# The recurrent branch's output product as seven products of halves, with its tokens kept in quads and its weight sums formed in DRAM

## The chip, the cores and the metric

The kernel runs on one core of a Trainium2 chip. It computes one decoder block for 512 tokens, and its time is the device time of one execution in microseconds. Before the change the median of three runs is 703.79 us (703.75 to 704.28).

Five engines work side by side, each on its own list of instructions in a fixed order: PE (TensorE, matrix products), DVE (VectorE), ACT (ScalarE), POOL (GpSimd) and SP (SyncE, which here only issues transfers). An instruction waits at the head of its engine's list until what it needs is there, and all behind it wait too. Transfers (DMAs) are issued by an engine and then run on their own. Matrix products read their operands from SBUF and write to PSUM, which has eight banks of 128 x 512 numbers.

## The reference

Only the part of the block up to the first residual sum is touched:

```python
h = rms_norm(x, g_mix_pre)
z = h @ w_in                       # (512, 1024) @ (1024, 4608): pool, rnn x, rnn gate, two gates
y_pool = pool_mixer(u_pool, pool_w, pool_scale) @ w_pool_out         # 512 -> 1024
y_rnn = rg_lru_branch(u_rx, u_rg, ...) @ w_rg_out                    # 1024 -> 1024
merged = gate_pool * y_pool + gate_rnn * y_rnn
x = x + rms_norm(merged @ w_o, g_mix_post)
```

`rg_lru_branch` ends with `h * gelu(gb)`, a scan's output times a gate. After this part come the feed-forward network (`w_up`, a short convolution, `w_down`) and a per-layer embedding. All is in float32.

## The kernel before, in words

**Precision.** PE multiplies in a shorter format (fp32r) than float32, so each operand is split into two: `hi`, a copy of it that ACT casts, and `lo`, the remainder that DVE subtracts (`split`, L190 and L194; L435 for weights that stream in). A product is three products, hi x hi, hi x lo and lo x hi, into one bank (`mm3`, L220 to L222).

**Layout.** A tile is 128 x 512 numbers: 128 channels by all 512 tokens. A weight tile of 512 KB (128 x 1024) serves one product of 128 output channels over 1024 inputs: eight blocks by three matmuls of 512 columns, 24 in all.

**Seven products of halves.** The products with `w_o`, `w_up` and `w_down` are already done so that a product of 2 x 2 blocks takes seven block products in place of eight. The sums of weight blocks that this needs (forms 5, 6, 7 and 4; forms 1, 2 and 3 are plain blocks) are made in DRAM: POOL issues a copy of a block to a sum tensor and then a transfer that adds another block to it (`sums_of`, `sum_in_dram`, L295). The sums of activations are DVE subtractions.

**Stages around the change.** The in-projection's last 24 steps (`IN_ORDER`) are 16 gate tiles, four pool tiles and four small maps. Then a loop over m = 0 to 7 makes, for 128 output channels each, `y_pool @ w_pool_out` (12 matmuls, key `wpo`) and `y_rnn @ w_rg_out` (24 matmuls, key `wrg`), and three DVE instructions (L879 to L881) multiply both by their gates and add them. Then the products with `w_o` follow, in the order of `SERIAL`.

**What sets the order.** PE's order is that of the program. The other engines' lists are laid by a scheduler from the program and from priorities (`urgent` puts an instruction ahead of others). Weights stream through six buffers each for `raw`, `hi` and `lo`; `weight` starts a tile's load, cast and subtraction four tiles ahead of its use. All loads are issued by SP, in one list.

**Early splits.** Ten weight tiles that are used later (six of `w_o`, four of `w_up`) are loaded, split and written back to DRAM as `parts` ahead of time (`split_early`), and read back when needed: one at each of the in-projection's last four steps (`EARLY_AT` = 20), and one in each of the loop's first six passes. Each takes a 512 KB load and two 512 KB writes on SP's list, a cast on ACT, a subtraction on DVE, and a `hi` and a `lo` buffer that come free when the writes have landed.

## Time and profile before

| | |
|---|---|
| median of the runs | 703.79 us |
| profiled execution: span / its own time | 702.1 us / 703.83 us |
| PE busy | 696.5 us (99%) |
| DVE busy / ACT busy / POOL busy | 574.1 / 440.9 / 82.9 us |
| moved by DMA | 172.54 MB |

The span runs from the first to the last instruction in the profile; 1.73 us lie around it. Times of day in what follows are microseconds from the span's start. The last gate tile ends and the loop over m begins at 203 us; the products with `w_o` begin at 265 us. A busy time is the time in which an engine has an instruction under way; matmuls overlap, so the distance between two starts, not the length of one, is the price of a matmul in a row of them.

### The profile page before, as it was taken

The numbers are of one execution on the slowest core, as the hardware profiler recorded it, in microseconds if no ns is written. First come the engines' busy times: TensorE is split into PE (matmuls) and PEld (weight loads), VectorE is DVE, ScalarE is ACT, GpSimd is POOL, SyncE is SP. The second block draws the span as 40 slices with busy tenths as digits, with TensorE's granted clock in tenths as the row PEclk, the third lists the DMA queues.
The fourth block names the chain that finished last, engine by engine and source line by source line (L and its number), as shares of the span: only waits on it lengthen the run. The fifth ranks groups of instructions, "written<-read, shape, count | busy, mean of one in ns | idle before, by whom it ended". The sixth has DMA issues, their size and how long they took to land.

```text
span 702.1 us, 11239 instructions
## 1 busy us (share of the span) xinstructions
PE 696.5 (99%) x4279; PEld 637.0 (91%) x4279; DVE 574.1 (82%) x749; ACT 440.9 (63%) x670; POOL 82.9 (12%) x107
## 2 busy tenths in 40 slices
PE   9999999999999999999999999999999999999997
PEld 8888888888888888899999999999999888888886
DVE  5698645999656568777989999997999999788972
ACT  6857789953543245468866667765767766665631
POOL 0221111110000000121013232121300000001100
PEclk9999999999999999999999999999999999999999
DMA  8999986656698999996479999998976577868111
GB/s 320 406 314 244 227 229 153 157 165 219 237 327 285 323 334 374 332 317 218 152 286 240 278 297 266 304 239 299 241 200 233 203 250 235 283 206 273 47 61 60
DMA packets 65077, 172.54 MB, mean 246 GB/s; under 512 B 5952, under 2 KB 6592, under 8 KB 64704
## 3 DMA queue, kind: packets, MB, share of 16 engines
q1 hardware_dynamic: 50480, 129.88, 53.2%
q0 software_dynamic: 14400, 41.95, 25.5%
q8 instruction: 33, 0.54, 0.3%
q14 instruction: 20, 0.16, 0.1%
q10 hardware_dynamic: 144, 0.00, 0.0%
HBM read 155.03 MB, written 58.72 MB: 304 GB/s over the span
## 4 chain that ended last, share of the span: by engine, by line
PE 99%; DVE 0%; ACT 0%; issue 0%
PE ps L220 31%; PE ps L222 31%; PE ps L221 31%; PE ps L541 3%; PE ps L913 1%; PE ps L650 1%; PE ps L239 1%; PE ps L592 0%; ACT t L165 0%; DVE t L1323 0%; DVE t L1324 0%; PE ps L1034 0%; DVE m L231 0%; DVE mhalf L233 0%
## 5 line engine op out<-in xcount | busy, mean ns | idle before, releaser
L190 DVE TENSOR_TENSOR lo<-raw,hi 128x1024 fp32r<-128x1024 f32 (+2 forms) x193 | 224.0, 1184 | 60.2 <-ACT hi L435 42.3
L220 PE MATMUL ps<-A,hi 128*128 128x256 f32 (+1 forms) x608 | 194.4, 320 | 0.0
L221 PE MATMUL ps<-A,hi 128*128 128x256 f32 (+1 forms) x608 | 193.8, 319 | 0.0
L222 PE MATMUL ps<-A,lo 128*128 128x256 f32 (+1 forms) x608 | 193.8, 319 | 0.0
L435 ACT CAST hi<-raw 128x1024 fp32r<-128x1024 f32 (+1 forms) x112 | 112.0, 1011 | 80.6 <-PE ps L222 27.6
L220 PEld LDWEIGHTS ps<-A,hi 128*128 128x128 f32 x608 | 115.9, 191 | 8.2 <-issue 1.0
L222 PEld LDWEIGHTS ps<-A,lo 128*128 128x128 f32 x608 | 116.0, 191 | 6.8
L221 PEld LDWEIGHTS ps<-A,hi 128*128 128x128 f32 x608 | 116.0, 191 | 6.8
L220 PE MATMUL ps<-C,hi 128*128 128x256 f32 (+1 forms) x392 | 114.5, 292 | 0.0
L222 PE MATMUL ps<-C,lo 128*128 128x256 f32 (+1 forms) x392 | 114.3, 292 | 0.0
L221 PE MATMUL ps<-C,hi 128*128 128x256 f32 (+1 forms) x392 | 114.3, 292 | 0.0
L194 ACT CAST hi<-raw 128x1024 fp32r<-128x1024 f32 x78 | 80.3, 1050 | 24.5 <-PE ps L221 14.5
L220 PE MATMUL ps<-hi,A 128*128 128x512 f32 x224 | 85.2, 380 | 0.0
L221 PE MATMUL ps<-lo,A 128*128 128x512 f32 x224 | 84.9, 379 | 0.0
L222 PE MATMUL ps<-hi,A 128*128 128x512 f32 x224 | 84.9, 379 | 0.0
L220 PEld LDWEIGHTS ps<-C,hi 128*128 128x128 f32 x392 | 74.7, 191 | 1.9
L221 PEld LDWEIGHTS ps<-C,hi 128*128 128x128 f32 x392 | 74.7, 191 | 1.8
L222 PEld LDWEIGHTS ps<-C,lo 128*128 128x128 f32 x392 | 74.7, 191 | 1.7
L462 POOL TENSOR_TENSOR s<-s,mhalf 128x1 f32<-128x1 f32 (+1 forms) x21 | 16.2, 773 | 336.9 <-DVE s L478 315.1
L220 PEld LDWEIGHTS ps<-hi,A 128*128 128x128 f32 x224 | 42.3, 189 | 6.3 <-ACT hi L435 0.3
L222 PEld LDWEIGHTS ps<-hi,A 128*128 128x128 f32 x224 | 42.3, 189 | 6.0
L221 PEld LDWEIGHTS ps<-lo,A 128*128 128x128 f32 x224 | 42.3, 189 | 5.8
(191 smaller groups left out, 1024.0 us busy)
## 6 DMA issues: line engine op xcount, KB each, us to landing
raw<-in_w_up_dram SPq DMA_DIRECT2D x46, 512.0 KB, 7.7
wdsum<-in_w_down_dram POOLq DMA_DIRECT2D x36, 512.0 KB, 9.2
raw<-in_w_in_dram SPq DMA_DIRECT2D x32, 512.0 KB, 6.9
raw<-wdsum SPq DMA_DIRECT2D x24, 512.0 KB, 4.5
raw<-in_w_down_dram SPq DMA_DIRECT2D x18, 512.0 KB, 4.0
wosum<-in_w_o_dram POOLq DMA_DIRECT2D x12, 512.0 KB, 9.0
wdsum<-wdsum POOLq DMA_DIRECT2D x12, 512.0 KB, 6.9
parts<-hi SPq DMA_DIRECT2D x10, 512.0 KB, 5.0
```

Of the source, the lines that this page charges most:

```text
L190: return V.tensor_tensor(o, a, b, ALU.subtract)
L194: last_copy[0] = ACT.copy(hi, src)
L220: PE.matmul(o, ah, bh, start=start, stop=False, **kw)
L221: PE.matmul(o, ah, bl, start=False, stop=False, **kw)
L222: PE.matmul(o, al, bh, start=False, stop=stop, **kw)
L239: PE.matmul(wps[:, :P], ones, ones, start=True, stop=True)
L435: ins = ACT.copy(hi, raw)
L462: last_pow[0] = nc.gpsimd.tensor_tensor(y, v, mhalf[:, :n], ALU.pow).ins.name
L541: PE.matmul(rx[m], a[:, o : o + P], turns(b), start=k == 0 and i == 0, stop=k == KD - 1 and i == 2)
L650: PE.matmul(ps, bd[pr, a, o], turns(b[pr]), start=i == 0, stop=i == 2)
L913: PE.transpose(ps[:, q * P : (q + 1) * P], a[:, q * P : (q + 1) * P], ident)
```

## The change

The product `y_rnn @ w_rg_out` becomes seven products of halves. Tokens are halved (256 each), and the output's 1024 channels are handled in two passes p = 0, 1 of 512. In each pass seven forms are multiplied, in the order `RSEVEN`; a form is two products (i = 0, 1) of four blocks by three matmuls of 256 columns, so that a pass has 168 matmuls. The weight tiles of forms 5, 6, 7 and 4 come from 16 more transfers on POOL's list, put ahead of those for `w_o`; the sums of p = 1, 2 of `w_up` are now issued side by side, as those of `w_rg_out` are.

The eight products with `w_pool_out` now stand in a row ahead of the fourteen forms. The output of the scan times its gate is written into two quads (`rgq`, four tiles each), and three DVE subtractions in them (`rg_sums`, at gate tiles 9 to 11) and one addition make the activation forms; forms 1 and 4 are split at gate tiles 5 and 8, the others in the `wpo` loop (`LATE_FORMS`). In PSUM the products collect in `rz`, `rd`, `ra` and `rb2`: ACT copies `rz` into `ra` and, negated, into `rb2` after forms 1, 6 and 7 (L938, L943, L945, L946), and `merge` does on DVE what L879 to L881 did, for halves.

Early splits start at step 15 in place of 20: nine lie in the in-projection's last nine steps, one in the `wpo` loop. The quarters of `w_o` take their input channels in another order, and the merged tokens lie in two quads `mq` to match. The two loads of `p_t` move from the loop's fourth pass to behind p = 0.

```diff
-EARLY_AT = 20
-SPLIT_AT = 5, 8
+EARLY_AT = 15
+FORMS_AT, RSUMS_AT = {5: 1, 8: 4}, (9, 10, 11)
...
+RSEVEN = (1, 5, 6, 2, 3, 7, 4)
...
+LATE_FORMS = {0: 5, 1: 6, 2: 3, 3: 7, 4: 2}
...
+    rsum = {(p, f): dram.tile([P, 2, S], F32, name=f"rg{p}sum{f}") for p in range(2) for f in (5, 6, 7, 4)}
...
+        if name in ("up", "rg"):
+            sums, of, ps = (usum, up_block, UP_SUMS) if name == "up" else (rsum, rg_block, range(2))
+            for fs in (((5, 11, 12), (7, 12, 22)), ((6, 5, 22),), ((4, 6, 21),)):
+                todo = [(p, *f) for f in fs for p in ps]
+                for p, f, start, _ in todo:
+                    yield sums[p, f], sums[p, start] if start < 10 else of(p, start), {}
+                for p, f, _, more in todo:
+                    yield sums[p, f], of(p, more), {"accum_op": ALU.add}
...
-    early = [("wo", f, q) for f in SERIAL[4:] for q in range(pieces["wo"])] + [("up", 0, f) for f in PLAIN]
+    early = [("wo", f, q) for f in SERIAL[4:] for q in range(pieces["wo"])]
+    early[2:2] = [("up", 0, f) for f in PLAIN]
...
-    sum_in_dram(chain_of(sums_of("wo"), sums_of("up")), None)
+    sum_in_dram(chain_of(sums_of("rg"), sums_of("wo"), sums_of("up")), None)
...
-            V.tensor_tensor(r_t[c], r_t[c], rg_t[c], ALU.mult)
+            V.tensor_tensor(rg_t[c], r_t[c], rg_t[c], ALU.mult)
...
+        w = quad("C" if f in (1, 2, 4) else "A").rearrange("p (s a) (b c) -> p s (a b) c", s=2, b=2)
+        split(w[:, 0], w[:, 1], v)
...
-    mq = [quad("A", F32), quad("A", F32)]
+    mq, pas = [], []
     for m in range(KD):
         w = weight(("wpo", m))
-        pa = bank()
+        if m in LATE_FORMS:
+            rg_form(LATE_FORMS[m])
+        if m == 6:
+            split_early(1)
+        pas.append(bank())
         for k in range(4):
-            mm3(pa, pick(w, k * P, (k + 1) * P), yp[k], k == 0, k == 3)
-        w = weight(("wrg", m))
...
-        for k in range(KD):
-            y = yh[k // 4][:, k % 4, :], yl[k // 4][:, k % 4, :]
-            mm3(pb, pick(w, k * P, (k + 1) * P), y, k == 0, k == KD - 1)
+            mm3(pas[m], pick(w, k * P, (k + 1) * P), yp[k], k == 0, k == 3)
...
+    def rg_product(p, f):
+        for i in range(2):
+            w = weight(("rg", p, f))
+            o = {1: rz, 6: rz, 7: rz, 2: ra, 4: ra, 3: rb2, 5: (rd, rd)}[f][i]
+            a = HALF if f == 4 or (f, i) == (5, 1) else 0
+            products(o[:, a : a + HALF], w, i, rform[f], f in (1, 5), turns)
+            z = rz[i][:, :HALF]
...
+                if f == 1:
+                    ACT.copy(ra[i][:, :HALF], z)
...
+                elif f == 7:
+                    ACT.copy(ra[i][:, HALF:], z)
+                    ACT.activation(rb2[i][:, HALF:], z, AF.Identity, scale=-1.0)
...
+    for p in range(2):
+        for f in RSEVEN:
+            if f == 2:
+                mq.append(quad("C", F32))
+            rg_product(p, f)
+            if (p, f) == (1, 6):
+                o_form(1)
+            if (p, f) == (1, 3):
+                o_form(2)
```

The change moves rows on SP, ACT and DVE. SP's list at the end of the in-projection and the start of the loop, first before: `parts` are the early tiles' writes, `raw` are loads.

```order
L428 DMA raw_1896<-in_w_rg_out_dram 128x1024
L428 DMA raw_1932<-in_w_pool_out_dram 128x512
L359 DMA parts_122<-hi_1848 128x1024
L359 DMA parts_122<-lo_1849 128x1024
L428 DMA raw_1951<-in_w_rg_out_dram 128x1024
L355 DMA raw_1957<-wosum_107 128x1024
L359 DMA parts_123<-hi_1890 128x1024
L359 DMA parts_123<-lo_1891 128x1024
L428 DMA raw_1993<-in_w_pool_out_dram 128x512
```

And the same place after, where raw_1823, raw_1865, raw_1907 and raw_1949 are the tiles of the `wpo` products m = 0 to 3:

```order
L373 DMA parts_133<-lo_1818 128x1024
L442 DMA raw_1823<-in_w_pool_out_dram 128x512
L369 DMA raw_1857<-wosum_106 128x1024
L442 DMA raw_1865<-in_w_pool_out_dram 128x512
L369 DMA raw_1899<-wosum_106 128x1024
L442 DMA raw_1907<-in_w_pool_out_dram 128x512
L373 DMA parts_134<-hi_1859 128x1024
L373 DMA parts_134<-lo_1860 128x1024
L373 DMA parts_135<-hi_1901 128x1024
L373 DMA parts_135<-lo_1902 128x1024
L369 DMA raw_1941<-wosum_107 128x1024
L442 DMA raw_1949<-in_w_pool_out_dram 128x512
```

The four writes of two early tiles and the load of a third now stand ahead of the load for m = 3, where before one tile's two writes stood between loads.

ACT's list at the end of the last gate tile, after: m_1938 and m_1980 are the last two gates' sigmoids, A_1989 and A_2012 forms 5 and 6, hi_1943 an early tile's cast, and hi_1951 the cast for m = 3.

```order
L166 ACTIVATE m_1938<-m_1938 128x512
L195 CAST A_1989<-C_406 128x1024
L195 CAST A_2012<-C_405 128x1024
L166 ACTIVATE m_1980<-m_1980 128x512
L195 CAST hi_1943<-raw_1941 128x1024
L449 CAST hi_1951<-raw_1949 128x512
L449 CAST hi_1985<-raw_1983 128x512
```

Two casts of forms, a sigmoid and an early cast now stand ahead of the cast for m = 3. The last place is ACT's list where the `w_o` products begin, first before: L994 copies `oz` of form 1 into `o11`, and A_2515 is the cast of form 5.

```order
L194 CAST A_2420<-A_1931 128x1024
L994 COPY ps_2450<-ps_2448 128x512
L435 CAST hi_2497<-raw_2495 128x1024
L994 COPY ps_2451<-ps_2449 128x512
L194 CAST A_2515<-C_2513 128x1024
L435 CAST hi_2520<-raw_2518 128x1024
```

And after, from form 7 of p = 1 on (L945 and L946 are its copies, A_2588 the cast of form 2 for `w_o`, L1066 the former L994, A_2755 the cast of form 5):

```order
L945 COPY ps_2085<-ps_2167 128x256
L946 ACTIVATE ps_2133<-ps_2167 128x256
L195 CAST A_2588<-C_2515 128x1024
L945 COPY ps_2105<-ps_2168 128x256
L946 ACTIVATE ps_2153<-ps_2168 128x256
L449 CAST hi_2699<-raw_2697 128x1024
L449 CAST hi_2724<-raw_2722 128x1024
L1066 COPY ps_2085<-ps_2692 128x512
L449 CAST hi_2737<-raw_2735 128x1024
L195 CAST A_2755<-C_2753 128x1024
L1066 COPY ps_2105<-ps_2693 128x512
```

The casts of forms 2 and 5 now stand between two copies, where before the cast of form 2 stood ahead of both and that of form 5 behind both.

More of the change, by code (lines that the diff above doesn't have):

```diff
@@ L37 @@
 SEVEN_1 = (1, 6, 2, 5, 7, 4)
+RSEVEN = (1, 5, 6, 2, 3, 7, 4)
 PLAIN = (11, 21, 12, 22)
-PLE_AT = 3
+LATE_FORMS = {0: 5, 1: 6, 2: 3, 3: 7, 4: 2}
 SERIAL = (1, 2, 5, 6, 3, 7, 4)
@@ L252, in block_kernel @@
     quarters = {
-        name: w.rearrange("(q a s p) c -> q s p a c", a=2, s=2, p=P) for name, w in (("wo", w_o), ("wd", w_down))
+        "wo": w_o.rearrange("(s q a p) c -> q s p a c", s=2, a=2, p=P),
+        "wd": w_down.rearrange("(q a s p) c -> q s p a c", a=2, s=2, p=P),
     }
@@ L272, in up_block, with rg_block @@
         return w_up[j : j + 2, :, h * S : (h + 1) * S].rearrange("j p c -> p j c")
+    def rg_block(p, f):
+        j, h = 4 * p + 2 * (f % 10 - 1), f // 10 - 1
+        return w_rg_out[j : j + 2, :, h * S : (h + 1) * S].rearrange("j p c -> p j c")
+    rsum = {(p, f): dram.tile([P, 2, S], F32, name=f"rg{p}sum{f}") for p in range(2) for f in (5, 6, 7, 4)}
     usum = {(p, f): dram.tile([P, 2, S], F32, name=f"up{p}sum{f}") for p in UP_SUMS for f in (5, 6, 7, 4)}
     def sums_of(name):
-        if name == "up":
-            for p in UP_SUMS:
-                for f, start, more in ((5, 11, 12), (7, 12, 22), (6, 5, 22), (4, 6, 21)):
-                    yield usum[p, f], usum[p, start] if start < 10 else up_block(p, start), {}
-                    yield usum[p, f], up_block(p, more), {"accum_op": ALU.add}
+        if name in ("up", "rg"):
[6 more added lines that the diff above has]
+                    yield sums[p, f], of(p, more), {"accum_op": ALU.add}
             return
@@ L325, in block_kernel @@
         plan(("wpo", m), w_pool_out[m])
-        plan(("wrg", m), w_rg_out[m])
+    for p in range(2):
+        for f in RSEVEN:
+            plan(("rg", p, f), rsum[p, f] if (p, f) in rsum else rg_block(p, {1: 11, 2: 21, 3: 22}[f]))
     for f in SERIAL:
@@ L442, in prep @@
                 behind(ins, last_low[0])
+        if key[0] == "rg":
+            hi, lo = (v.rearrange("p (j c) -> p j c", j=2) for v in (hi, lo))
         ready[key] = (hi, lo)
@@ L679, in rnn_decay @@
             V.tensor_tensor_scan(r, a_t[c], r, 0.0, ALU.mult, ALU.add)
-    yh = [None, None]
-    yl = [None, None]
     def rnn_out(cs):
@@ L686, in rnn_out, with rg_half, rg_sum, rg_form @@
             act(rg_t[c], rg_t[c], AF.Gelu_apprx_tanh)
-            V.tensor_tensor(r_t[c], r_t[c], rg_t[c], ALU.mult)
-    def rnn_split(i):
-        yh[i], yl[i] = quad("C"), quad("C")
-        for q in range(4):
-            split(yh[i][:, q, :], yl[i][:, q, :], r_t[4 * i + q])
+            V.tensor_tensor(rg_t[c], r_t[c], rg_t[c], ALU.mult)
+    rform = {}
+    def rg_half(k, b):
+        return rgq[k][:, :, b * HALF : (b + 1) * HALF]
+    def rg_sum(o, a, b, op=ALU.subtract):
+        V.tensor_tensor(rg_half(*o), rg_half(*a), rg_half(*b), op)
+    def rg_form(f):
+        if f == 3:
+            rg_sum((0, 0), (0, 0), (1, 0), ALU.add)
+        v = rg_half(*{1: (0, 0), 2: (1, 0), 4: (1, 1), 5: (1, 1), 6: (0, 0), 3: (0, 0), 7: (0, 1)}[f])
+        w = quad("C" if f in (1, 2, 4) else "A").rearrange("p (s a) (b c) -> p s (a b) c", s=2, b=2)
+        split(w[:, 0], w[:, 1], v)
+        rform[f] = w[:, 0], w[:, 1]
+    def rg_sums(n):
+        rg_sum(*(((1, 1), (0, 1), (1, 1)), ((0, 1), (0, 0), (0, 1)), ((0, 0), (1, 1), (0, 0)))[n])
     banks = list(rx)
@@ L766, in gate_tile @@
         gate[m] = g
-        if m in SPLIT_AT:
-            rnn_split(SPLIT_AT.index(m))
+        if m in FORMS_AT:
+            rg_form(FORMS_AT[m])
+        if m in RSUMS_AT:
+            rg_sums(RSUMS_AT.index(m))
     for n, step in enumerate(IN_ORDER):
@@ L837, in o_form @@
     def o_form(f):
-        h11, h12, h21, h22 = (halves(mq[k], b) for b in range(2) for k in range(2))
+        h11, h12, h21, h22 = (halves(mq[k], b) if k < len(mq) else None for b in range(2) for k in range(2))
         v = {1: h11, 2: h12, 4: h22}.get(f)
@@ L860, in o_lhs, with products @@
         return v[:, 0], v[:, 1]
-    mq = [quad("A", F32), quad("A", F32)]
+    def products(o, w, i, form, start, order=near):
+        for k in range(4):
+            lhs = tuple(v[:, i, k * P : (k + 1) * P] for v in w)
+            rhs = tuple(v[:, k, :] for v in form)
+            mm3(o, lhs, rhs, start and k == 0, k == 3, order, skip_group_check=True)
+    mq, pas = [], []
     for m in range(KD):
         w = weight(("wpo", m))
-        pa = bank()
-        for k in range(4):
-            mm3(pa, pick(w, k * P, (k + 1) * P), yp[k], k == 0, k == 3)
-        w = weight(("wrg", m))
-        if m == KD - 1:
-            o_form(1)
-        split_early(1)
-        pb = bank()
-        for k in range(KD):
-            y = yh[k // 4][:, k % 4, :], yl[k // 4][:, k % 4, :]
-            mm3(pb, pick(w, k * P, (k + 1) * P), y, k == 0, k == KD - 1)
-        a, b = gate[m], gate[8 + m]
-        with urgent():
-            V.tensor_tensor(row(a), back(pa), row(a), ALU.mult)
-            V.tensor_tensor(row(b), back(pb), row(b), ALU.mult)
-            V.tensor_tensor(mq[m % 2][:, m // 2, :], a, b, ALU.add)
-        if m == KD - 1:
-            o_form(2)
-        if m == PLE_AT:
+        if m in LATE_FORMS:
[3 more added lines that the diff above has]
+        pas.append(bank())
+        for k in range(4):
+            mm3(pas[m], pick(w, k * P, (k + 1) * P), yp[k], k == 0, k == 3)
+        with urgent():
+            V.tensor_tensor(row(gate[m]), back(pas[m]), row(gate[m]), ALU.mult)
@@ new lines, in block_kernel, with merge @@
+    rz, rd, rq = [bank(), bank()], bank(), {}
+    ra, rb2 = pas[4:6], pas[6:8]
+    def merge(p, n, i, hs):
+        m, c = 4 * p + 2 * n + i, hs.stop - hs.start
+        g, v = gate[8 + m][:, hs], (ra, rb2)[n][i][:, hs]
+        with urgent():
+            if n:
+                t = temp()[:, :c]
+                q = rq[p][:, None, i * HALF : (i + 1) * HALF].to_broadcast([P, c // HALF, HALF])
+                V.tensor_tensor(*(x.rearrange("p (h c) -> p h c", c=HALF) for x in (t, v)), q, ALU.add)
+                v = t
+            g4 = g.rearrange("p (h a b) -> p h a b", a=2, b=P)
+            V.tensor_tensor(g4, v.rearrange("p (h b a) -> p h a b", a=2, b=P), g4, ALU.mult)
+            V.tensor_tensor(mq[p][:, 2 * n + i, hs], gate[m][:, hs], g, ALU.add)
@@ new lines, in rg_product @@
+    def rg_product(p, f):
[5 more added lines that the diff above has]
+            z = rz[i][:, :HALF]
+            with urgent():
+                if f == 1:
+                    ACT.copy(ra[i][:, :HALF], z)
+                elif (f, i) == (5, 1):
+                    rq[p] = temp()
+                    ACT.copy(rq[p], rd)
+                elif f == 6:
+                    ACT.activation(rb2[i][:, :HALF], z, AF.Identity, scale=-1.0)
+                elif f == 7:
+                    ACT.copy(ra[i][:, HALF:], z)
+                    ACT.activation(rb2[i][:, HALF:], z, AF.Identity, scale=-1.0)
+            if p and f in (2, 3):
+                merge(p, int(f == 3), i, slice(0, HALF))
+            elif f in (7, 4):
+                merge(p, int(f == 7), i, slice(HALF * p, S))
@@ L885, in block_kernel @@
+    for p in range(2):
+        for f in RSEVEN:
+            if f == 2:
[5 more added lines that the diff above has]
+                o_form(2)
+        if p == 0:
             pled = dram.tile([S, D], F32, name="pled")
@@ L949, in h2 @@
         return tuple(v[c][b] for v in (h2h, h2l))
-    def products(o, w, i, form, start):
-        for k in range(4):
-            lhs = tuple(v[:, i, k * P : (k + 1) * P] for v in w)
-            rhs = tuple(v[:, k, :] for v in form)
-            mm3(o, lhs, rhs, start and k == 0, k == 3, near, skip_group_check=True)
     def up_plain(f, b):
@@ L981, in x2_out @@
                 V.scalar_tensor_tensor(h2n[t, h], res[h], r, g_pre[h], ALU.mult, ALU.mult)
-    oz, o11, o12, od5 = ([bank(), bank()] for _ in range(4))
+    o11, o12 = ra, rb2
+    oz, od5 = ([bank(), bank()] for _ in range(2))
     o5 = wpool.tile([P, 2, S], F32, tag="sum", name=nm("sum"), bufs=1)
```

## The prediction

> **What bounds the kernel now.** I read the page's busy times and chain first.

> ```profile
> PE 696.5 (99%) x4279; PEld 637.0 (91%) x4279; DVE 574.1 (82%) x749; ACT 440.9 (63%) x670; POOL 82.9 (12%) x107
> PE 99%; DVE 0%; ACT 0%; issue 0%
> ```

> PE is the bound from end to end, so a matmul removed is worth its price, as long as nothing makes PE wait. The price is the distance between two starts. PE's timeline shows it for the product that goes, and for 256 columns in a product that already has the new form:

> ```profile
> 240.20 0.38 PE L220 MATMUL ps<-C,hi 128*128 128x512 f32 x1
> ...
> 241.06 0.38 PE L221 MATMUL ps<-C,hi 128*128 128x512 f32 x1
> ...
> 353.18 0.28 PE L221 MATMUL ps<-C,hi 128*128 128x256 f32 x1
> ...
> 353.62 0.28 PE L222 MATMUL ps<-C,lo 128*128 128x256 f32 x1
> ```

> Four steps of 512 columns take 0.86 us, 0.2157 each (the rows between are as far apart); four of 256 take 0.44, 0.1115 each over a longer row. Next, what the other engines have left, by stretches (PE, PEld, DVE, ACT, POOL busy, granted clock, DMA share, GB/s):

> ```profile
> 27.00:110.00 83.00, 83.00 (x407) 70.78 (x406) 61.58 (x107) 60.19 (x81) 17.02 (x20) 1.00 0.93 259
> 110.00:157.00 47.00, 47.00 (x219) 41.15 (x219) 40.77 (x69) 37.62 (x58) 8.07 (x10) 1.00 0.66 167
> 157.00:170.00 13.00, 13.00 (x62) 11.39 (x61) 12.99 (x22) 3.62 (x5) 0.10 (x1) 1.00 0.71 222
> 170.00:180.00 10.00, 10.00 (x48) 8.68 (x48) 9.58 (x16) 6.45 (x10) 0.00 (x0) 1.00 0.48 159
> 180.00:190.00 10.00, 10.00 (x48) 8.77 (x47) 7.11 (x10) 5.43 (x8) 0.00 (x0) 1.00 0.76 261
> 190.00:203.00 13.00, 13.00 (x62) 11.39 (x61) 7.18 (x8) 5.56 (x7) 0.00 (x0) 1.00 0.98 351
> 203.00:224.00 21.00, 21.00 (x99) 18.38 (x98) 12.21 (x16) 9.61 (x13) 0.00 (x0) 1.00 0.88 306
> 224.00:240.00 16.00, 16.00 (x76) 14.00 (x75) 10.15 (x14) 5.25 (x7) 0.00 (x0) 1.00 0.90 300
> ```

> DVE has nothing free in 157 to 170, and the DMA engines are idle for some share only until 190. The transfers' own rows (queue: packets, MB, share; then issues, with KB and median us to landing), and a wait in which a weight's cast stands behind an early tile's write:

> ```profile
> q1 hardware_dynamic: 50480, 129.88, 53.2%
> q0 software_dynamic: 14400, 41.95, 25.5%
> raw<-wosum SPq DMA_DIRECT2D x8, 512.0 KB, 6.8
> parts<-hi SPq DMA_DIRECT2D x10, 512.0 KB, 5.0
> raw<-in_w_pool_out_dram SPq DMA_DIRECT2D x8, 256.0 KB, 4.1
> ACT hi L435 <- DMA parts<-hi: 20.8, 5, 5.9
> ```

> That wait comes five times, up to 5.9 us, and PE doesn't notice: the weights stood ready early enough. This reserve is what the change spends.

> **The change part by part.**

> *Matmuls.* Removed: 8 x 8 x 3 = 192 of 512 columns, 192 x 0.2157 = 41.4 us. Added: 2 x 7 x 2 x 4 x 3 = 336 of 256, 336 x 0.1115 = 37.5 us. Net -3.95 us with PE dense. The row of 353 us includes a weight load for each matmul, hidden. [...]

> *Gate and merge work* (DVE, ACT). Halves in place of wholes: more instructions of half the size, in 203 to 265, where DVE has 9 of 21 and 6 of 16 us free. Nothing by itself; two places where PE waits for such a piece come below. The three subtractions at gates 9 to 11 are another matter. Rows for the pieces (DVE, ACT; the second number is the mean ns):

> ```profile
> L1180 DVE TENSOR_TENSOR C<-h,h 128x1024 f32<-128x1024 f32 x3 | 3.7, 1218 | 0.0
> L190 DVE TENSOR_TENSOR lo<-raw,hi 128x512 fp32r<-128x512 f32 x10 | 6.9, 687 | 12.2 <-ACT hi L435 7.5 <-ACT m L165 3.8 <-ACT hi L432 0.9
> L435 ACT CAST hi<-raw 128x1024 fp32r<-128x1024 f32 x103 | 106.7, 1045 | 58.2 <-PE ps L222 27.6 <-DMA parts<-hi 13.0 <-PE ps L221 8.2
> L1048 ACT COPY ps<-ps 128x256 f32<-128x256 f32 x22 | 7.9, 358 | 28.5 <-PE ps L222 28.5
> 159.80 0.69 DVE L190 TENSOR_TENSOR m<-t,m 128x512 fp32r<-128x512 f32 x1
> 164.66 0.38 PE L221 MATMUL ps<-m,hi 128*128 128x512 f32 x1
> ```

> The last two are pool group 1's `lo` (ready 160.5) and the map that reads it (164.66): 4.2 us in hand. The three subtractions (3 x 1.22 = 3.7) and one weight's `lo` (1.22) now stand ahead of it: 4.9. So the map starts 0.7 late, or, if they run 0.1 us closer each (instructions in a row overlap), 0.3. I take 0.4; bounds 0 (each of the two splits of four 512 pieces becomes one of 1024, which saves 4 x 0.69 - 1.22 = 1.5 ahead of it) and 1.2 (one more `lo` ahead).

> *Early splits, the main cost.* Nine lie in 165 to 203, where four lay in 182 to 203. Each is three transfers on SP's queue. Several casts in that stretch can't start before an early tile's write has landed, which the waits in ACT's list tell. Laying it out by rows: gate 8's sigmoid, ahead of the first early cast, follows its evacuation:

> ```profile
> 170.22 0.69 DVE L606 TENSOR_TENSOR m<-ps,rb 128x512 f32<-128x512 f32 x1
> ```

> Two to three us later with the added DVE work, so first early cast at 174. From there a hop is a cast and a write, 1.05 + 5.0 = 6.05, and three hops hang together: to 180 (gate 10's weight, then two early casts between sigmoids, at 183 and 185), to 189 (second early tile's write, then the fourth's cast), to 196 (fourth's write, then the sixth's cast). Its `lo` (1.2) and write stand on SP ahead of the load for m = 0: issued at 198. It lands 4.1 later, its cast and `lo` add 1.3: ready at 203.4, against PE at 203.1. Then a round: an early tile's load (6.8), two casts of 1024 and one of 512 (2.7), its `lo` (1.2), writes issued (0.5), load for m = 3 behind an early load (4.1), the early cast and its own cast and `lo` (1.05 + 0.62 + 0.69): 17.7, so m = 3 is ready at 215.7. A `wpo` product is 12 x 0.2157 = 2.6 us, so PE, 0.4 and 0.3 late, wants it at 203.1 + 0.7 + 7.8 = 211.6. The stall is 4.1, with the 0.3 some 4.4; I take 4.3. Bounds: with 4.1, the quickest of the rows, for every write and load, three hops and the round are 5.4 shorter, and nothing is left: 0. With 5.9 for a hop's write (the longest wait) and as much again for the m = 3 load: 8. Before, m = 1's load shows the same wait with time in hand:

> ```profile
> 190.87 0.76 SPq L428 DMA_DIRECT2D raw<-in_w_pool_out_dram  x1
> 196.90 0.62 ACT L435 CAST hi<-raw 128x512 fp32r<-128x512 f32 x1 [2.77 <-DMA parts<-hi]
> ```

> Ready at 198 for a use at 211; now its place in PE's list is 205.7. That six splits leave the loop is no gain: PE didn't wait there.

> *Transfers.* 16 sums at 4.27 us a MB (0.255 x 702.1 / 41.95) and 0.524 MB are 35.8 us of all 16 DMA engines; six more weight tiles at 2.88 (0.532 x 702.1 / 129.88) are 9.1. Free in 27 to 240 by the shares above: 5.8 + 16.0 + 3.8 + 5.2 + 2.4 + 0.3 + 2.5 + 1.6 = 37.6. Short by 7.3, which the sums of `w_up` can take after 240. Nothing by itself, and a rival below. The new sums are ready long before use: first on POOL's list, 16 sums take 55 us.

> ```profile
> 24.15 1.57 POOL L295 DMA_DIRECT2D wosum<-in_w_o_dram  x2
> 79.13 1.04 POOL L295 DMA_DIRECT2D wosum<-in_w_o_dram  x1 [3.35 <-DMA wosum<-wosum]
> 156.07 1.03 POOL L295 DMA_DIRECT2D up2sum<-in_w_up_dram  x1 [3.56 <-DMA up2sum<-up2sum]
> ```

> *Copies between banks.* Form 6 adds to `rz`, so it waits for form 1's copies (0.36 each). Between lie form 5's 24 matmuls, 2.7 us; the second copy stands on ACT behind two casts of weights, each of which waits for a buffer that PE frees. 0.9, the wait of one cast; bounds 0 (casts ready) and 1.9 (two casts behind the freeing). Form 4 of p = 1 needs form 7's second copy, behind the cast of form 2 for `w_o`, which waits for merges on DVE. From the end of form 3, merge 3 x 0.4 (an estimate for 256 columns, from 0.69 for 512), cast 1.05, copy 0.36 with 0.3 of draining make 2.9 to 3.0, against 24 matmuls, 2.68: 0.3; one `lo` of 1.22 ahead on DVE makes 1.5. I take 1.1, since DVE is 10 of 16 busy there and the merges of form 4 queue as well. At the `w_o` products a cast of form 5 now precedes the second copy; before:

> ```profile
> 270.18 0.57 ACT L994 COPY ps<-ps 128x512 f32<-128x512 f32 x1 [0.19 <-PE ps L222]
> 270.67 1.05 ACT L194 CAST A<-C 128x1024 fp32r<-128x1024 f32 x1
> ```

> Copy done at 270.75; its bank is wanted six matmuls (1.3) after 270.2, so 0.75 in hand against 1.05: 0.3, and 1.3 if DVE's form 5 is late by a `lo`; I take 0.5.

> Sum: -3.95 + 0.4 + 4.3 + 0.9 + 1.1 + 0.5 = +3.25. Against the profiled execution's 703.83 (span 702.1 and 1.73 around it), which stands 0.04 above the median, 707.1 us. All ends low: 700.5; all high, 714.

> **The rivals.**

> *The early splits stay hidden, and it is faster.* Speaks for it: in 170 to 190 the DMA share is 0.48 and 0.76, so writes there may land in 4 us, not 5. Against: 190 to 203 is at 0.98 already, with four early tiles. Without the 4.3 and with the copies between low and taken: -3.95 + 0.4 + 1.5 = -2.0, 701.8 us. It decides at m = 3's weight: ready by 211.6 or not.

> *DMA engines full.* The sums then push SP's transfers from 157 on. For it: short by 7.3 us until 240, and with some 2 us free between 240 and the first load of a `w_up` sum at 267 (a share of 0.92 there), 5.3 are left for PE. -3.95 + 5.3 + 4.3 + 2.9 = +8.5, 712.3 us. [...]

> *256 columns not at half price*, with weight loads bare. A load takes 637.0 / 4279 = 0.149 us on the page; 336 of them exposed make 50 us more, 750 us. The row at 353 us excludes it but for 1 in 100.

> **How the numbers follow.** 0.2%, 1.4 us, is about what a measurement of this kernel can tell from no change: 702.4 to 705.2. The forecast as summed, 705.2 to 710, has 0.5; full DMA engines 0.15; the 1 in 100 aside, hidden splits have 0.23 and what falls between 0.11. So slower 0.66, same 0.11, faster 0.23. The range runs from 701.5, inside the faster case, to 712.5; the forecast's own is 705 to 710.

> **What would show it.** Right: PE idle of some 3 to 5 us between 203 and 217, ended by a cast or `lo` of a `wpo` weight; about 1 us each before form 6 of p = 0, and at the end of p = 1, ended by ACT's copies; 256-column starts 0.11 apart. Wrong: no idle at m = 3, writes of `parts` landing in 4 us; or gaps over all of 157 to 240 with a DMA share of 0.98, which is the second rival. The map's 0.4 stands at 165.

## The result, and the profile after

The changed kernel takes 715.73 us (median; 714.36 to 716.38), the kernel before beside it 704.03 (703.75 to 704.75). The ratio is 1.0162, with a 95% interval of 1.0143 to 1.0181: slower by 11.7 us where 3.3 were forecast. The profiled execution has 715.15 us of its own, a span of 713.4, 11.3 more than before. The page's busy times, its chain, and its row of the early tiles' writes (KB, median us to landing):

```profile
PE 698.2 (98%) x4423; PEld 639.2 (90%) x4423; DVE 592.1 (83%) x772; ACT 455.8 (64%) x693; POOL 96.0 (13%) x123
...
PE 77%; DVE 10%; ACT 5%; DMA 4%; issue 3%; SPq 1%; DVEq 0%; ACTq 0%
...
parts<-hi SPq DMA_DIRECT2D x10, 512.0 KB, 3.8
```

PE carried 99% of the chain, and now carries 77%. The rest of the chain runs through the splitting of weights: DVE's remainders, ACT's casts, and transfers. What PE waited for (total us, times, longest), from the list of waits:

```profile
PE ps L221 <- ACT hi L449: 5.8, 2, 4.5
PE ps L222 <- DVE m L191: 1.3, 2, 0.7
...
PE ps L221 <- ACT ps L945: 1.0, 1, 1.0
PE ps L223 <- DVE lo L191: 0.8, 2, 0.6
PE ps L221 <- ACT ps L1066: 0.3, 1, 0.3
```

They add up to 9.2 us, less than the loss, and L1066 is the former L994. The rest is in the stretches (columns as in the prediction: PE, PEld, DVE, ACT, POOL busy, granted clock, DMA share, GB/s):

```profile
110.00:157.00 47.00, 47.00 (x219) 41.16 (x218) 40.79 (x64) 34.70 (x51) 13.21 (x16) 1.00 1.00 258
157.00:170.00 13.00, 12.27 (x57) 10.43 (x56) 12.92 (x23) 3.36 (x5) 3.00 (x4) 1.00 1.05 307
170.00:180.00 10.00, 9.47 (x45) 7.97 (x44) 8.43 (x15) 3.50 (x5) 2.25 (x3) 1.00 0.90 225
180.00:190.00 10.00, 10.00 (x48) 8.77 (x47) 5.17 (x7) 5.77 (x8) 0.00 (x0) 1.00 0.77 226
190.00:203.00 13.00, 13.00 (x62) 11.39 (x61) 9.24 (x10) 7.23 (x9) 0.00 (x0) 1.00 1.03 415
203.00:224.00 21.00, 14.30 (x54) 10.30 (x53) 14.35 (x18) 12.97 (x18) 0.00 (x0) 0.90 0.96 336
224.00:240.00 16.00, 16.00 (x85) 14.25 (x84) 15.24 (x17) 8.68 (x10) 0.00 (x0) 0.91 0.95 351
```

Three things differ from before. The DMA engines, idle for 0.34, 0.29 and 0.52 of their time in 110 to 180, are now nearly full there, POOL's last sums among it (3.0 and 2.3 us of POOL's time in 157 to 180, before 0.1). PE is busy in only 14.3 of 21 us from 203 on. And the granted clock, 1.00 in each of these stretches before, is 0.90 and 0.91 in the last two. PE's timeline shows where that comes from; these matmuls are of the `wpo` product m = 3:

```profile
219.48 0.48 PE L221 MATMUL ps<-m,hi 128*128 128x512 f32 x1 [4.47 <-ACT hi L449]
...
220.82 0.79 PE L223 MATMUL ps<-m,lo 128*128 128x512 f32 x1 [0.57 <-DVE lo L191]
...
222.26 0.63 PE L223 MATMUL ps<-m,lo 128*128 128x512 f32 x1
222.69 0.63 PE L221 MATMUL ps<-m,hi 128*128 128x512 f32 x1
...
227.10 0.38 PE L223 MATMUL ps<-m,lo 128*128 128x512 f32 x1
227.32 0.38 PE L221 MATMUL ps<-m,hi 128*128 128x512 f32 x1
```

After a wait of 4.47 us and another of 0.57, the matmuls start 0.43 apart until 226.5, twice the 0.2157 of before and of 227.1 on: the clock had halved (the granted clock is 0.50 from 219.97 to 226.80), and cost 3.04 us. The prediction had no term for that.

The whole loss, from PE's starts: for every matmul of either trace, the distance to the next start above 0.2157 (0.1115 for 256 columns), after minus before.

| term of the prediction's sum | forecast | measured |
|---|---|---|
| matmuls | -3.95 | -3.99 |
| maps | +0.4 | +1.82 |
| weights of `wpo`, m = 0 to 3 | +4.3 | +8.28 (2.73 for m = 0 to 2, 5.55 for m = 3) |
| half clock behind m = 3's wait | 0 | +3.04 |
| copy ahead of form 6 | +0.9 | +0.28 |
| copy ahead of form 4 of p = 1 | +1.1 | +1.29 |
| copy at the `w_o` products | +0.5 | +0.61 |
| sum | +3.25 | +11.33 |

From 300 us on the two traces run in parallel. Most of the loss lies at m = 0 to 3, and the view of the chain shows how it came about (start, length, what; "issue" is time for which the profile names nothing; `parts` are early tiles' writes, L449 casts a tile that is used next, and the L195 casts here are of early tiles):

```profile
173.20 1.04 ACT hi L195
174.26 3.09 DMA parts<-hi
177.35 3.47 issue
180.82 0.13 ACT hi L449
...
200.77 4.35 DMA raw<-in_w_pool_out_dram
...
211.77 6.03 DMA raw<-wosum
...
217.87 1.05 ACT hi L195
```

This is the chain that was forecast, link by link: the first early cast (forecast at 174, here 173.2), gate 10's cast behind its write (180, here 180.8), the load for m = 0 (198, here 200.8), m = 3 (215.7, here 219.5 and, with its remainder, 220.8). The links were longer than priced. Two stand out. From the first write to gate 10's cast go 6.5 us. The view gives 3.1 of them to the write and names nothing for 3.5; but by its own row that write has 6.5 us from issue to landing, so that it lands at 180.76, and the cast starts at 180.82: the whole link is the write. And m = 3's cast stood on ACT's list behind an early tile's, whose load took 6.0 us. Its own load, issued 1.1 us after that one, took 5.6 and landed at 218.46, so that at 218.82 the cast started only 0.4 us after it could have: both loads were slow.

### The profile page after: what moved, and what is told of

The parts are those of the page before. It is cut to its first block, busy times and chain, and to the rows that moved or that the text cites. A ratio compares the mean times of both kernels' runs of the same rounds, so it can differ in the third digit from the quotient of the medians.

```text
span 713.4 us, 11625 instructions
## 1 busy us (share of the span) xinstructions
PE 698.2 (98%) x4423; PEld 639.2 (90%) x4423; DVE 592.1 (83%) x772; ACT 455.8 (64%) x693; POOL 96.0 (13%) x123
## 4 chain that ended last, share of the span: by engine, by line
PE 77%; DVE 10%; ACT 5%; DMA 4%; issue 3%; SPq 1%; DVEq 0%; ACTq 0%
PE ps L221 25%; PE ps L223 24%; PE ps L222 24%; DVE lo L191 3%; PE ps L557 2%; ACT m L166 2%; DVE m L695 1%; ACT t L166 1%; PE ps L990 1%; DMA parts<-hi 1%; DMA raw<-in_w_rx_dram 1%; DMA raw<-wosum 1%; ACT hi L449 1%; PE ps L666 1%; ACT hi L195 1%
## 5 line engine op out<-in xcount | busy, mean ns | idle before, releaser
L191 DVE TENSOR_TENSOR lo<-raw,hi 128x1024 fp32r<-128x1024 f32 (+2 forms) x199 | 230.8, 1185 | 52.0 <-ACT hi L449 34.0
L221 PE MATMUL ps<-A,hi 128*128 128x256 f32 (+1 forms) x672 | 212.0, 316 | 0.0
L223 PE MATMUL ps<-A,lo 128*128 128x256 f32 (+1 forms) x672 | 211.4, 315 | 0.0
L222 PE MATMUL ps<-A,hi 128*128 128x256 f32 (+1 forms) x672 | 211.4, 315 | 0.0
L449 ACT CAST hi<-raw 128x1024 fp32r<-128x1024 f32 (+1 forms) x118 | 118.4, 1013 | 65.4 <-PE ps L223 27.6
L221 PEld LDWEIGHTS ps<-A,hi 128*128 128x128 f32 x672 | 128.2, 191 | 8.2 <-issue 1.0
L223 PEld LDWEIGHTS ps<-A,lo 128*128 128x128 f32 x672 | 128.3, 191 | 6.9
L222 PEld LDWEIGHTS ps<-A,hi 128*128 128x128 f32 x672 | 128.2, 191 | 6.8
L221 PE MATMUL ps<-C,hi 128*128 128x256 f32 x376 | 103.7, 276 | 1.0 <-ACT ps L945 1.0
L223 PE MATMUL ps<-C,lo 128*128 128x256 f32 x376 | 103.2, 274 | 0.0
L222 PE MATMUL ps<-C,hi 128*128 128x256 f32 x376 | 103.2, 274 | 0.0
L195 ACT CAST hi<-raw 128x1024 fp32r<-128x1024 f32 x78 | 80.6, 1050 | 23.4 <-PE ps L222 18.3
L221 PE MATMUL ps<-hi,A 128*128 128x512 f32 x224 | 85.4, 381 | 0.3 <-ACT ps L1066 0.3
L222 PE MATMUL ps<-lo,A 128*128 128x512 f32 x224 | 84.9, 379 | 0.0
L221 PEld LDWEIGHTS ps<-C,hi 128*128 128x128 f32 x376 | 71.8, 191 | 1.6 <-ACT ps L945 1.4
L222 PEld LDWEIGHTS ps<-C,hi 128*128 128x128 f32 x376 | 71.8, 191 | 0.1
L221 PEld LDWEIGHTS ps<-hi,A 128*128 128x128 f32 x224 | 42.3, 189 | 7.0 <-ACT ps L1066 0.7
L306 POOL DMA_DIRECT2D wdsum<-in_w_down_dram x36 | 33.3, 1087 | 109.8 <-ACT ps L1113 53.2
## 6 DMA issues: line engine op xcount, KB each, us to landing
raw<-in_w_up_dram SPq DMA_DIRECT2D x46, 512.0 KB, 8.0
wdsum<-in_w_down_dram POOLq DMA_DIRECT2D x36, 512.0 KB, 9.7
raw<-in_w_in_dram SPq DMA_DIRECT2D x32, 512.0 KB, 8.0
raw<-wdsum SPq DMA_DIRECT2D x24, 512.0 KB, 4.3
raw<-in_w_down_dram SPq DMA_DIRECT2D x18, 512.0 KB, 4.2
wosum<-in_w_o_dram POOLq DMA_DIRECT2D x12, 512.0 KB, 8.9
wdsum<-wdsum POOLq DMA_DIRECT2D x12, 512.0 KB, 7.8
parts<-hi SPq DMA_DIRECT2D x10, 512.0 KB, 3.8
```

Source lines behind the costliest of these rows:

```text
L191: return V.tensor_tensor(o, a, b, ALU.subtract)
L195: last_copy[0] = ACT.copy(hi, src)
L221: PE.matmul(o, ah, bh, start=start, stop=False, **kw)
L222: PE.matmul(o, ah, bl, start=False, stop=False, **kw)
L223: PE.matmul(o, al, bh, start=False, stop=stop, **kw)
L306: ins = nc.gpsimd.dma_start(o, i, **kw)
```

## The experiments

The theory after the result: the dense early splits hold up the casts of weights that are needed at once, and the wait that PE gets then halves its clock. Rivals: the 16 new sums fill the DMA engines, and without them the same splits would be hidden; the loads only stand behind the writes on SP's list; the clock falls for the work of the other engines, not for PE's wait. All edits are to the changed kernel, but for the last pair. The same kernel before ran beside each, with medians of 704.15 to 704.46.

**The old places for the early splits.** They start at step 20 again; the other five go between forms of the new product.

```diff
-EARLY_AT = 15
+EARLY_AT = 20
+EARLY_RG = (0, 1), (0, 6), (0, 3), (0, 4), (1, 5)
...
             rg_product(p, f)
+            if (p, f) in EARLY_RG:
+                split_early(1)
```

> Early splits start at step 20 again, so that five in place of ten are made by the end of the product with w_pool_out, and the other five follow in the fourteen forms of the recurrent product. Theory A (packed early splits: the loads for w_pool_out stand on SP behind writes that wait for casts and buffers): the waits at m = 0 to 3 (8.3 us in the changed kernel) and the half clock after them (3.0 us) go, 704.4 us, or up to 706 if the five moved ones make new waits. Theory B (the 16 added sums fill the DMA engines): nothing of that is touched, 713 us or more.

722.46 us, 1.0267 (1.0234 to 1.0300). At m = 0 to 3 nothing waits any more. Its stretch 203 to 224:

```profile
203.00:224.00 21.00, 21.00 (x99) 18.38 (x98) 18.92 (x23) 13.74 (x17) 0.00 (x0) 1.00 0.70 235
```

And from the timeline the largest wait that came instead, with ACT's list ahead of it (lines are one higher than in the changed kernel, so L196, L450 and L946 are its L195, L449 and L945):

```profile
240.94 1.05 ACT L196 CAST hi<-raw 128x1024 fp32r<-128x1024 f32 x1 [1.42 <-DMA parts<-hi]
...
244.60 1.04 ACT L450 CAST hi<-raw 128x1024 fp32r<-128x1024 f32 x1 [2.62 <-DMA raw<-rg1sum]
245.56 0.37 ACT L946 COPY ps<-ps 128x256 f32<-128x256 f32 x1
...
245.97 0.38 PE L222 MATMUL ps<-C,hi 128*128 128x256 f32 x1 [2.98 <-ACT ps L946]
```

So the density of the early splits makes the waits at m = 0 to 3. But among the forms the splits hurt more: a form's copy between banks, which PE needs at once, stands on ACT behind casts that wait for a write and for a load. More waits follow at the `w_o` products, of 1.2 at 272 and of 1.4 and 2.2 at 282 to 285, ended there by remainders on DVE and by a weight's cast, and the clock halves at 246 and at 285 (256 columns start 0.21 apart from 246.78 on, 512 columns 0.43 apart from 285.83). The product that left had taken 24 x 0.2157 = 5.2 us for each 512 KB of weights; a form takes 24 x 0.1115 = 2.7.

**PE kept busy ahead of m = 3.** Twenty more matmuls, whose results the product then overwrites.

```diff
         pas.append(bank())
+        if m == 3:
+            for k in range(20):
+                PE.matmul(pas[m], ht(k % KD)[0][:, :P], ht(k % KD)[0], start=True, stop=True)
```

> Twenty matmuls of 512 columns (4.3 us) whose result is thrown away stand ahead of the m = 3 product, where PE waits 4.6 us. Theory C (the granted clock falls because PE stood idle for 4.5 us): matmuls after the gap keep 0.2157 us instead of 0.43, 3 us less, 712.7 us, and the granted clock is 1.00 in 203 to 240. Rival D (the clock falls for another reason, such as the work of the other engines): no gain, 715.7 us or more, clock 0.90 there.

719.84 us, 1.0212 (1.0195 to 1.0229). Its two stretches:

```profile
203.00:224.00 21.00, 17.50 (x73) 12.89 (x72) 13.01 (x16) 10.77 (x15) 0.00 (x0) 1.00 0.87 307
224.00:240.00 16.00, 16.00 (x96) 14.58 (x95) 12.43 (x15) 8.44 (x9) 0.00 (x0) 1.00 0.86 308
```

And ACT's list where it lost the time again (L941 copies `rz` after form 1):

```profile
243.89 1.99 ACT L449 CAST hi<-raw 128x1024 fp32r<-128x1024 f32 x2 [6.62 <-issue]
...
245.79 0.36 ACT L941 COPY ps<-ps 128x256 f32<-128x256 f32 x1
```

The clock stays at 1.00 and no matmul here runs at half speed; by 240 PE has done 169 - 20 = 149 matmuls of the kernel where the changed one has done 139. That supports the half clock as a term of its own. The time didn't follow: with more matmuls in the program the scheduler laid the lists otherwise. An early tile's write now stands on SP behind two more loads, is issued at 238.4 where in the changed kernel at 232.3, and lands at 243.8. The two casts ahead of a form's copy start only then, and PE waits 5.4 us for the copy at 246, at half clock afterwards (256 columns start 0.21 apart from 246.58 on). The expected time was missed for a reason outside the question.

**Without the new sums.** The 16 sums are left out, and forms 5, 6, 7 and 4 multiply plain blocks; so these four forms of the output product have other weights, and the same number of matmuls and loads.

```diff
-            plan(("rg", p, f), rsum[p, f] if (p, f) in rsum else rg_block(p, {1: 11, 2: 21, 3: 22}[f]))
+            plan(("rg", p, f), rg_block(p, {1: 11, 2: 21, 3: 22, 5: 12, 6: 11, 7: 12, 4: 21}[f]))
...
-    sum_in_dram(chain_of(sums_of("rg"), sums_of("wo"), sums_of("up")), None)
+    sum_in_dram(chain_of(sums_of("wo"), sums_of("up")), None)
```

> The 16 sums of w_rg_out are left out and the forms 5, 6, 7 and 4 of the recurrent product read plain blocks, so that these four forms are multiplied by other weights than they should be; all else is as in the changed kernel. Theory A: SP's transfers in 165 to 215 get quicker by up to 1 us each, and the chain of hops shrinks by 2 to 5 us, 709 to 713 us. Theory B (DMA engines full): nearly all of the loss goes, 701 to 705 us.

710.18 us, 1.0083 (1.0062 to 1.0104). Two of its stretches:

```profile
170.00:180.00 10.00, 9.47 (x44) 7.99 (x43) 9.17 (x19) 3.76 (x7) 0.00 (x0) 1.00 0.40 141
...
203.00:224.00 21.00, 18.03 (x75) 14.88 (x74) 16.56 (x21) 13.02 (x19) 0.00 (x0) 0.92 0.96 340
```

And PE at m = 3:

```profile
217.27 0.48 PE L221 MATMUL ps<-m,hi 128*128 128x512 f32 x1 [2.32 <-ACT hi L449]
...
218.61 0.71 PE L223 MATMUL ps<-m,lo 128*128 128x512 f32 x1 [0.64 <-DVE lo L191]
219.11 0.63 PE L221 MATMUL ps<-m,hi 128*128 128x512 f32 x1
```

The sums cost 715.73 - 710.18 = 5.6 us. Without them the DMA share in 170 to 180 is 0.40, not 0.90; the first early write lands in 2.6 us and is followed by gate 10's cast within 3.0 (176.92 to 179.91), not 6.5; and m = 0 to 2 don't wait. At m = 3 3.4 us are left, with half a clock behind them (starts 0.43 apart from 219.11 to 222.10). (The profiled execution is the slowest of the four, 711.85 us: it lost 2.6 us ahead of 16 us from the span's start, before any sum is issued, and its times of day are later by that.) So the splits are not hidden without the sums, but nearly half of the loss hangs on them.

**The writes issued by POOL.** SP's list then holds loads only.

```diff
-                nc.sync.dma_start(parts[key][i], v.bitcast(F32))
+                nc.gpsimd.dma_start(parts[key][i], v.bitcast(F32))
```

> The early tiles' writes are issued by POOL in place of SP, the same transfers in the same number, so that loads no longer stand behind writes that wait for a cast. Theory A: the loads for m = 0 to 3 go out 5 us or more earlier, the waits there and the half clock go for the most part, 705 to 708 us; what is left is the wait for buffers. Theory B: the DMA engines carry the same bytes, 713 us or more.

726.08 us, 1.0326 (1.0290 to 1.0363). The writes, from the page:

```profile
parts<-hi POOLq DMA_DIRECT2D x10, 512.0 KB, 5.7
```

And gate 10's cast on ACT:

```profile
185.86 1.04 ACT L449 CAST hi<-raw 128x1024 fp32r<-128x1024 f32 x1 [8.32 <-issue]
```

The first write stands behind the last sums on POOL, is issued at 176.75 and not at 174.26, and lands 9.0 us later, at 185.79, just ahead of the cast at 185.86; the median of the writes is 5.7 us, not 3.8. The load for m = 0 does go out earlier, at 196.1 and not at 200.8, that for m = 2 later, at 206.2 and not at 204.0. PE's waits between 190 and 236 add up to 13.4 us, in the changed kernel to 6.7. So taking the writes off SP's list gave no relief: casts wait until writes have landed and their buffers are free. What loads on SP would have gained with writes that land as fast as before, this run can't tell.

**The three subtractions later,** behind pool group 3's remainder, so that no pool group's remainder stands behind them on DVE.

```diff
-        V.tensor_tensor(rg_half(*o), rg_half(*a), rg_half(*b), op)
+        ins = V.tensor_tensor(rg_half(*o), rg_half(*a), rg_half(*b), op)
+        if len(pool_low) == 4:
+            behind(ins, pool_low[3])
```

> The three DVE subtractions that form the recurrent tokens' sums stand behind the last pool group's lo instead of ahead of group 1's. Theory: the two waits of the maps (0.90 and 0.70 us, with the restarts 1.8 us in all) are due to these subtractions and go; the early chain starts a little sooner. 713 to 714.2 us, no PE wait at 165 and 172. Rival: the maps wait because DVE is full there whatever stands first; 715.7 us.

715.64 us, 1.0152 (1.0116 to 1.0189). The maps' 1.82 us are gone, as expected (0.02 left); the expected gain in time did not come. PE, earlier by as much, meets the early splits: new waits of 0.6 and 0.8 at 193, and 3.0 in place of 1.35 at m = 0, with half clock behind it (starts 0.43 apart from 208.50 to 211.06). While the chain holds, this gain ahead of it is worth nothing.

**One early split per gate tile,** none at pool tiles or maps.

```diff
-        split_early(1 if n >= EARLY_AT else 0)
+        split_early(1 if n in EARLY_STEPS else 0)
...
+EARLY_STEPS = 11, 13, 15, 17, 19, 20, 21, 22, 23
```

> The nine early splits of the in-projection are laid one to each gate tile (gates 7 to 15), where the changed kernel makes one at each map as well from gate 9 on. Theory A (the chain of casts, writes and buffers is too dense): with 5 us and more between two of them the waits at m = 0 to 3 shrink to 1 us or none and PE keeps its full clock after them, 704 to 706 us. Rival (what counts is how many bytes the DMA engines move until 215 us): the same bytes, 713 us or more.

722.04 us, 1.0244 (1.0221 to 1.0267). No wait at m = 0 to 3, but one of 8.8 us before. From the list of PE's waits:

```profile
PE ps L221 <- ACT m L195: 11.1, 2, 8.8
```

And the cast on ACT ahead of the awaited one:

```profile
190.29 1.04 ACT L449 CAST hi<-raw 128x1024 fp32r<-128x1024 f32 x1 [7.53 <-DMA parts<-lo]
```

Started earlier, the splits run into the sums of `w_up` (DMA share 1.04, 1.02 and 1.05 in 157 to 190), their writes land late, and a pool group's cast, which PE needs at once, stands on ACT behind a weight's cast that waits for such a write.

**All three shifts together:** the last two, and the casts of forms 2 and 5 for `w_o` behind the copies between banks.

```diff
         split(of[f][:, 0], of[f][:, 1], v)
+        if f in (2, 5):
+            behind(last_copy[0], o_copied[f == 5])
...
-            if (p, f) == (1, 3):
+            if (p, f) == (1, 7):
                 o_form(2)
```

> One early split to a gate tile, the subtractions behind the pool groups, and the casts of forms 2 and 5 for w_o behind the copies that stood behind them. If the waits of the changed kernel are those named, and no other takes their place, 3.95 us are left as gain: 700 to 701.5 us. If a chain of buffers or the DMA engines only move the waits elsewhere: 705 us or more.

723.86 us, 1.0275 (1.0244 to 1.0306). The waits at the copies of 270 to 300 are gone, so that order does what it should; one of 1.1 comes at 307. The splits' waits remain: 3.9 at a map, 1.2 at 201, 3.3 at m = 3, 6.7 at a form's copy at 250.

**No early splits:** every tile is split when it is used.

```diff
-    early[2:2] = [("up", 0, f) for f in PLAIN]
+    early = []
```

> No early splits at all: the ten tiles are loaded and split where they are used, as all other weights are. Theory A: the waits at m = 0 to 3 and the half clock behind them go (11 us less); what the early splits were for comes back in the products with w_o and the first of w_up, where twenty reads of parts become ten loads, casts and subtractions: up to 10 us more there. Rival (the waits at m = 0 to 3 come from the sums alone): they stay.

711.72 us, 1.0105 (1.0088 to 1.0123). Nothing waits at m = 0 to 3, with a granted clock of 1.00 in 203 to 240, and up to 284 us PE stands 0.4 us behind the kernel before. Then waits come where there were none: 0.9 at 297, ended by DVE, and

```profile
324.66 0.38 PE L221 MATMUL ps<-C,hi 128*128 128x256 f32 x1 [3.52 <-ACT m L824]
```

for a copy on ACT that stands behind squares, which had waited 3.3 us for DVE. That these come from the splits that weren't made is argued from their place; the next run, with the four tiles of `w_up` split early, has the first of them and not the second. So early splits pay later on, and ten as dense as these cost more earlier.

**Four early splits in place of ten,** those of `w_up`, one at each of the last four steps; first alone, then with the later subtractions and the casts behind the copies.

```diff
-EARLY_AT = 15
+EARLY_AT = 20
...
-    early[2:2] = [("up", 0, f) for f in PLAIN]
+    early = [("up", 0, f) for f in PLAIN]
```

> The four early tiles of w_up alone as in e10_four_all, without the two changes of order. Theory: as there, with the maps' 1.8 us and the copies' 1.8 us left in: 704 to 706 us; no wait at m = 0 to 3 and full clock in 203 to 240. Rival: 708 us or more.

> Only the four tiles of w_up are split early, one at each of the last four steps of the in-projection as in the kernel before; the six of w_o are loaded and split where they are used. Besides, the subtractions stand behind the pool groups and the casts of forms 2 and 5 behind the copies. Theory (early splits and the order of DVE's and ACT's rows are what costs, not the seven products): no wait left but 0.25 us before form 6 and about 1 us in the w_o products, 700.5 to 702.5 us, faster than the kernel before. Rival (the 16 added sums slow SP's transfers whatever is done with the splits): 704 us or more.

Alone 705.61 us, 1.0016 (1.0007 to 1.0026): no wait at m = 0 to 3, and the granted clock is 1.00 from 157 to 360. What is left are the maps (1.8), the copies, and the 0.9 at 297. With both orders 702.64 us, 0.9978 (0.9969 to 0.9987), 1.8 us faster than the kernel before, and just above the 700.5 to 702.5 expected. Its stretch from 203:

```profile
203.00:224.00 21.00, 21.00 (x101) 18.42 (x100) 17.54 (x22) 14.06 (x18) 0.00 (x0) 1.00 0.67 227
```

And its largest wait behind the first products, at `w_o`:

```profile
283.12 0.45 PE L221 MATMUL ps<-hi,A 128*128 128x512 f32 x1 [0.71 <-ACT A L195]
```

The two orders are worth 3.0 us here, and the one tried alone on the changed kernel 0.1: their gain arrives only once the chain behind them is gone. How the kernel before would run with four early splits wasn't tried, so 0.9978 is not the product's gain alone.

**PE made to wait, in the kernel before.** One small matmul at m = 1 waits for a copy on ACT and one (three) subtractions on POOL.

```diff
         pa = bank()
+        if m == 1:
+            idle = temp()
+            ACT.copy(idle, pb)
+            for _ in range(1):
+                nc.gpsimd.tensor_tensor(idle, idle, idle, ALU.subtract)
+            PE.matmul(pa[:, :P], idle[:, :P], idle[:, :P], start=True, stop=True)
```

> The kernel before, with PE held idle once ahead of the m = 1 product of w_pool_out: ACT copies the bank just written, POOL subtracts the copy from itself once, and a small matmul that is thrown away reads the result. Theory C (an idle PE loses its clock only after an idle time between 2 and 2.7 us): if the gap is under 2 us, matmuls behind it keep 0.2157 us and the time grows by the gap alone. Rival D (any break halves the clock): 0.43 us for some microseconds.

> The same with three subtractions on POOL in a row, for a gap of about three times the length. Theory C: if the gap is over 2.7 us, matmuls behind it take 0.43 us for 2.5 to 6 us, so that the time grows by the gap and another 1.3 to 3 us. Rival D' (the half clock in the changed kernel had to do with the load of DMA, ACT and DVE there): 0.2157 us right behind the gap, and the time grows by the gap alone.

714.92 us, 1.0148 (1.0122 to 1.0174), and 718.65, 1.0201 (1.0179 to 1.0223). PE with three subtractions:

```profile
221.30 0.80 PE L872 MATMUL ps<-t 128*128 128x128 f32 x2 [9.94 <-POOL t L871]
...
222.32 0.63 PE L221 MATMUL ps<-m,hi 128*128 128x512 f32 x1
222.75 0.63 PE L222 MATMUL ps<-m,lo 128*128 128x512 f32 x1
```

Twelve matmuls start 0.43 apart here (222.32 to 227.01), thirteen in the changed kernel, and with one subtraction (7.65 us idle) six. A wait of PE is enough, in a kernel whose other engines do what they did: the rival of the other engines' work falls. The short case came out at 8 us, not at the 2 or so that would have shown where the effect begins, so Theory C's 2 to 2.7 us stay an estimate.

## Why the prediction was right and wrong

**Right:** slower; that PE's waits would come at the maps, at m = 0 and 3 and at the three copies, and behind which instructions; the matmuls (-3.99 against -3.95, so that 256 columns are half the price, 0.1115 to 0.2157); the copies, 2.2 in place of 2.5. The outcome, 715.73, lies above the range's 712.5.

**Wrong, first: "Transfers ... Nothing by itself".** The sum of free shares in 27 to 240 had the new sums fit but for 7.3 us, and priced the loss at nothing, with full DMA engines as a rival for 0.15. The run without the sums shows 5.6 us for them; the rival's own price was 5.3. They don't push SP's loads everywhere, as that rival had it. They move the later sums into 157 to 175, where the first links of the chain are, and lengthen these: 6.5 us from write to cast with them, 3.0 without; the write itself took 6.5 and 2.6. (That the engines are idle for some share only until 190 was misread as well: the rows before have 0.12 and 0.10 idle from 203 to 240, and the sum counts them.) A total of free shares doesn't tell how long the transfer that heads a chain takes.

**Second, the same step seen from the chain: "so first early cast at 174 ... m = 3 is ready at 215.7".** It was ready at 220.8, 5.1 later. 2.8 of that had come up by the load for m = 0 (200.8, not 198). 1.9 are one link of the round: I put 4.1, the quickest of the rows, for the load ahead of the last two casts, and the early tile's load took 6.0 (m = 3's own 5.6). With PE 3.8 us later itself than forecast (1.4 at the maps, 2.4 at m = 0 to 2), this turns the 4.0 forecast at m = 3 into 4.0 + 5.1 - 3.8 = 5.3; 5.55 were measured. The 4.3 for the term is nearer to the kernel without the sums, with its 3.4 at m = 3.

**Third, a term that was missing: the clock.** The sum priced a wait of PE at its length. This one of 4.85 us, start to start, cost another 3.04, since the matmuls behind it ran at half speed. The filled kernel and the two with a forced wait bear that out. The speed is the granted clock's: 0.43 for 0.2157, with 0.50 granted from 219.97 to 226.80. Which waits it followed is told below.

**Fourth, the maps: "I take 0.4".** Three of the four instructions ahead of group 1's remainder on DVE (another lies between), the remainder, and the first map, after:

```profile
157.08 1.22 DVE L709 TENSOR_TENSOR C<-C,C 128x1024 f32<-128x1024 f32 x1
...
162.46 1.22 DVE L709 TENSOR_TENSOR C<-C,C 128x1024 f32<-128x1024 f32 x1
163.59 1.21 DVE L191 TENSOR_TENSOR lo<-raw,hi 128x1024 fp32r<-128x1024 f32 x1
164.73 0.68 DVE L191 TENSOR_TENSOR m<-t,m 128x512 fp32r<-128x512 f32 x1
...
165.46 0.48 PE L222 MATMUL ps<-m,hi 128*128 128x512 f32 x1 [0.73 <-DVE m L191]
```

The remainder starts at 164.73, 4.9 us later than before, which is what the four instructions were added up to; the map then lost 1.0, near the 0.7 that the plain sum gave and that was rounded down. The other 0.8 come at the next map, at 172, for which the forecast had nothing: DVE stays late.

**Left open:** how the loss divides between the sums and the density, as the runs took away each by itself and the two do not add up; and why the loads at m = 3 were slow without the sums too (5.7 us for its own).

## What to carry to other kernels

A product that becomes shorter for PE needs its weights faster: a saving on the bound engine is to be set against what the others must now deliver in the shorter time, and work that prepares something for later is best thinned out first (ten early splits to four turned 715.7 us into 705.6). On an engine that works through its list in order, look at what stands ahead of the instruction that PE needs at once: a cast that waits for a transfer there costs PE that transfer, in each place to which a cast was moved here. And a wait of PE can cost more than its length: here 2.32 and 0.64 us of idle time close together were followed by half clock that cost 1.5 us (without the sums, 219.11 to 222.10), and 4.47 and 0.57 us by half clock that cost 3.04, while 1.35 and 1.56 us, each by itself, were followed by full clock.
